# A hybrid decoder step on one core: 54 tiles in the buffer pool in place of 53, and weights kept 4 casts and 3 splits ahead in two stages

## The chip, the cores and the metric

One NeuronCore of a Trainium2 chip. TensorE multiplies, VectorE (DVE) and ScalarE (ACT) do elementwise work, GpSimd (POOL) does little besides issuing DMAs, SyncE (SP) issues most of the loads. Each engine runs its instructions in the order in which they are written; semaphores order the engines among each other. The metric is the device time of one execution in microseconds (us), median of three.

## The reference

One step of a decoder on 1024 prompt tokens and 8 decoding tokens, width 2048, all float32: a pooling layer (A), a key and value projection shared by what follows, and a layer of sliding-window attention (B). Cut to what matters:

```python
def pool_layer(x, prefix, pos, w_in, w_grp, scale, w_out, g_ln, b_ln):
    z = x @ w_in                                    # 2048 -> 4096
    u, gate = z[..., :D_POOL], z[..., D_POOL:]
    d, new_state = multiscale_pool(u, prefix, pos)  # windows 2, 4, 8, 16
    d = jnp.einsum('btgc,gce->btge', d..., w_grp) * scale
    y = (d * jax.nn.silu(gate)) @ w_out
    return layer_norm(ALPHA * x + y, g_ln, b_ln), new_state

kv = h @ w_kv                                       # 4 heads x 64, shared

def attn_layer(x, ...):
    z = x @ w_in                                    # queries and gate
    o = attn_core(rope(q), kb, vb, ..., sinks)      # window 128, a sink per head
    y = (o * jax.nn.silu(gate)) @ w_out
    return layer_norm(ALPHA * x + y, g_ln, b_ln)
```

## The kernel before

**Stages.** The tokens are two chunks: chunk 0 of 512, chunk 1 of 520 (with the 8 decoding tokens). The stages run in the order ai0, ai1 (input of the pooling layer, by chunk), ao0, ao1 (its output), bi0, bi1 (input of the attention layer, with the attention itself woven in), bo0, bo1 (its output). In the profile ai0 lasts to about 388 us, ai1 to 757, ao0 to 914, ao1 to 1080, bi0 to 1536, bi1, the second attention stage, to 1975, bo0, the one behind it, to 2154, and bo1 to the end.

**Products.** A product by a weight block of 128 by 1024 is three matmuls for each of eight slices: a float32 number is split in a high part (ScalarE casts it, L476 for weights, L766 for activations) and a low part (VectorE subtracts, L491 and L775), and high·high (L655), high·low (L656) and low·high (L657) are summed in PSUM. The matmul at L657 is the only one that reads the low part of the weight. Most stages use a form with seven products of block sums in place of eight (Strassen's); the sums of weights are made by VectorE at L334 and written back by GpSimd's DMA (names `swia`, `swob` and so on), so that the second chunk loads them. Two stretches (the first of ai0 and the first of bi0) use plain products (L683 to L685, `unit`).

**Stream of weights.** All weight blocks form one list. Ahead of each product `begin()` writes into the queues what is due: `load_to` issues loads (on SP) up to a products ahead, `prep_to` the splits up to d ahead, `cast_to` the casts up to b ahead, `make_to` the sums that a cast needs. (a, b, d) is `self.ahead`, and 7, 4, 3 at first. From the last queries of bi1 (L2069) it is 6, 3, 2, until 23 products into bo0 (L2186), where it is 7, 4, 3 again. In bi1, whenever fewer than four tiles of the pool are whole and free, `begin()` itself takes 6, 3, 2.

**Pool.** `Mem` holds 53 tiles of 128 by 1040 float32. `full()` gives a whole tile, `half()` half of one, always the one that has been free longest. A weight, its high and its low part take a tile each, and so do pairs of activations.

**Side work.** What isn't a product of the stream is written between products by generators: `x_tick` loads, casts and splits the activations of the next stage, `sum_gen` makes sums of the weights of later stages (L424, L428, L429), others do layer norm (L1277, L1288, L1289), the residual (L1234) and attention. `x_tick` and `sum_gen` go by the number of free tiles: so the size of the pool sets where in the queues their instructions stand. The attention's scores are copied from PSUM (L1793, L1838), masked (L1797 with an int32 mask `mki`; L1839 with a float one in `cst`) and used by L1776, L1829, L1853. L594, L600, L603, L609, L615 and L628 are ScalarE's copies of finished products out of PSUM, L616 and L621 VectorE's.

**Constants.** `cst` holds an identity, a mask, a matrix of 1/D and reciprocal counts, loaded at the start in one DMA, with `mki`.

Of the kernel before, what the change touches and what calls it, by code (L numbers as in the profile page):

```python
# [46 lines left out]
K_ID, K_MP, K_J, K_RC = 0, 128, 256, 384  # L47
N_CST = 384 + 4 * NST
# [15 lines left out]
NSLOT = 53  # L64
# [71 lines left out]
class Mem:  # L136
# [21 lines left out]
    def half(self):  # L158
        part = [(a if b is None else b, i) for i, (a, b) in enumerate(self.f) if (a is None) != (b is None)]
        if part and min(part)[0] > self.clock - 6 and len(self.whole()) > 7:  # L160
            part = []
        i = min(part)[1] if part else min(self.whole(), key=lambda i: max(self.f[i]))
# [4 lines left out]
        return Slot(self, i, h, self.t[i][:, h * TMAX : (h + 1) * TMAX])  # L167
# [15 lines left out]
class Kern:  # L183
    def __init__(self, ctx, tc, io):
# [87 lines left out]
    def load1(self, s, k, src):  # L272
        def go():
            s[k] = self.mem.full()
            self.nc.sync.dma_start(s[k].a[:, :1024], src)

        return go
# [42 lines left out]
    def first_pair(self, name, q):  # L320
# [8 lines left out]
        def add(out, x, y, i):  # L329
            def go():  # L330
                assert self.prepped >= self.made - 2
                if out not in s:
                    s[out] = self.mem.full()
# [68 lines left out]
    def sum_gen(self, name):  # L402
# [8 lines left out]
        def load(n):  # L411
            if n < len(parts) and n not in held:
                q, cs = parts[n]
                s = held[n] = self.mem.full()
# [71 lines left out]
    def prep_to(self, n):  # L486
        self.cast_to(n)
        while self.prepped < min(n, len(self.stream)):
            s = self.stream[self.prepped]
            hi, lo = self.hl[self.prepped], self.mem.full()  # L490
# [76 lines left out]
    def seven(self, c, z0, z1, after, c11=None, split=False, own=None):  # L567
# [30 lines left out]
        def p2():  # L598
            o["s"] = self.mem.half()
# [122 lines left out]
    def t_first(self, j):  # L722
# [5 lines left out]
        if k == 0:  # L728
            for i in (1, 2, 3, 6):
                self.pre[i, g] = self.mem.full(), self.i  # L730
# [9 lines left out]
    def x_load(self):  # L740
# [4 lines left out]
        s = self.mem.full()  # L745
# [13 lines left out]
    def x_cast(self, k):  # L759
# [5 lines left out]
        h = self.mem.full()  # L765
# [3 lines left out]
    def x_make(self):  # L769
# [4 lines left out]
        l = self.mem.full()  # L774
# [42 lines left out]
    def t_ops(self, E, O, dst, kp, TH):  # L817

        nc = self.nc
        s = self.mem.full()  # L820
# [9 lines left out]
    def t_gen(self, key):  # L830
# [3 lines left out]
        def load(kp):  # L834
            s[kp] = self.mem.full()
# [14 lines left out]
    def j_steps(self, T, a, b, box, *free):  # L850

        def add():
            box["u"] = self.mem.half()
# [4 lines left out]
        def high():  # L858
            box["hl"] = self.mem.full()
            self.nc.scalar.copy(box["hl"].r[:, :T], box["u"].a[:, :T])  # L860

        def low():
            u, hl = box.pop("u"), box["hl"]
            self.nc.vector.tensor_sub(hl.r[:, TMAX : TMAX + T], u.a[:, :T], hl.a[:, :T])
# [4 lines left out]
    def j_sum(self, T, box, out):  # L869

        J, hl = self.jr[:], box.pop("hl")
        src = hl.r[:, :T], hl.r[:, TMAX : TMAX + T]
# [11 lines left out]
    def j_sum32(self, T, src, out):  # L884

        J = self.cst[:, K_J : K_J + P]
# [22 lines left out]
    def ln_gen(self, c, pre, acc, gc, bc, out, td):  # L909
# [6 lines left out]
        L = self.mem.full()  # L916
        mu, rr = L.a[:, :T], L.a[:, TMAX : TMAX + T]

        def load(p):
            if p < 8 and p not in pre:  # L920
                pre[p] = self.mem.full()
# [27 lines left out]
        w = self.mem.full()  # L949
        q, v = w.a[:, :T], w.a[:, TMAX : TMAX + T]  # L950
        if c == 0:
            nc.vector.tensor_mul(q, mu, mu)
        else:
            sq, sqs = self.mem.full(), {}
            for p in range(10):
# [4 lines left out]
                if 1 <= p <= 8:  # L960
                    sqs[p - 1] = sq if p == 1 else self.mem.full()
# [50 lines left out]
    def pool_tile(self, c, m, Us, ext, dd):  # L1012
# [13 lines left out]
        bufs = [self.mem.full() for _ in range(2 if w > 2 else 1)]  # L1026
# [10 lines left out]
        if c == 0:  # L1037
            o = K_RC + g * NST
# [15 lines left out]
        def rest():  # L1054
            d = self.mem.full()
            hl = d.r[:, :T], d.r[:, TMAX : TMAX + T]
# [7 lines left out]
    def group_half(self, c, g, h, dd, sg):  # L1064
# [30 lines left out]
        def post():  # L1095
            G = self.mem.full()
# [18 lines left out]
    def two(self, T):  # L1115
# [3 lines left out]
        def z(i):  # L1119
            def go():  # L1120
                if "s" not in box:
                    box["s"] = self.mem.full()
# [6 lines left out]
    def phase_ai(self, c, gs, nxt):  # L1129
# [4 lines left out]
        for g in gs:  # L1134
            ext = es = None
            if T > TP:
                es = self.mem.half()
# [3 lines left out]
            for i in range(4):  # L1141
                if not self.strassen:

                    def done(ps, i=i):
                        U = self.mem.full()
# [4 lines left out]
                elif i % 2 == 0:  # L1150
                    us = {}

                    def z(j, us=us):
                        def go():
                            us[j] = self.mem.full()
# [17 lines left out]
            for i in range(4):  # L1173
                if g == gs[-1] and i == 0:
                    self.x_begin(nxt)
                if not self.strassen:

                    def done(ps, i=i):
                        if i % 2 == 0:
                            sg[i // 2] = self.mem.full()  # L1180
# [1167 lines left out]
```

## Time and profile before

| what | value |
| --- | --- |
| median of three runs | 2343.66 us (2342.93 to 2345.91) |
| the profiled execution: its own time, its span | 2347.06 us, 2345.3 us |
| TensorE busy | 2303.4 us, 98% |
| VectorE, ScalarE, GpSimd busy | 1923.2 (82%), 1364.5 (58%), 204.1 (9%) |
| matmuls in all | 19960 |
| moved by DMA | 669.39 MB, mean 285 GB/s |

A row of a group reads: line, engine, operation, what is written <- what is read, shapes, xcount, then busy us and mean ns of one, then idle time of the engine just ahead of them and what ended most of it. `m` is any tile of the pool, `pD`, `pS`, `pO` are PSUM tiles. A row of waits reads: the engine and line that waited, what ended the wait, total us, times, longest. In a timeline the first number is the start, the second the duration, the bracket the idle time ahead.

### The profile page before, as it was taken

To read this page: it belongs to the slowest core of one execution; us is meant where nothing else is said; L and a number is where in the kernel's file an instruction comes from. 1 tells how busy PE (TensorE), PEld (TensorE's weight loads), DVE (VectorE), ACT (ScalarE), POOL (GpSimd) and SP (SyncE) were. 2 spreads that over 40 slices of the span, in tenths; PEclk is the share of its full clock that TensorE was granted. 3 is DMA by queue.
4 is the path that set the end of the run, shared out by engine and by line. 5 is a ranking of instruction groups with operands and counts; after the bars stand their busy time and mean duration, and the time that the engine had idled before them with its cause. 6 is when DMAs were issued, how large, how long until landed. Compare 5 with 4: busy or idle time off the path is not lost. (4 is left out here: it accounts for less than half of the span.)

```text
span 2345.3 us, 49654 instructions
## 1 busy us (share of the span) xinstructions
PE 2303.4 (98%) x19960; PEld 2204.5 (94%) x19960; DVE 1923.2 (82%) x2382; ACT 1364.5 (58%) x2502; POOL 204.1 (9%) x383
## 2 busy tenths in 40 slices
PE   8999999999999999999999999999999999999997
PEld 6899999999999999998787899999999999999997
DVE  8788898777878878868998898887777777888897
ACT  4454446544546557554464666685666768556666
POOL 0111110010000000000111111100000000000001
PEclk9999999999999999999999999999999999999999
DMA  7668789989889989999799766788776768699794
GB/s 295 211 242 309 269 289 343 339 281 323 297 297 334 321 289 331 316 337 331 260 327 360 256 229 227 246 290 273 251 253 227 240 201 289 228 354 370 264 343 173
DMA packets 252072, 669.39 MB, mean 285 GB/s; under 512 B 25760, under 2 KB 106560, under 8 KB 251840
## 3 DMA queue, kind: packets, MB, share of 16 engines
q1 hardware_dynamic: 206368, 501.14, 63.1%
q0 software_dynamic: 45472, 165.07, 18.1%
q8 instruction: 156, 2.56, 0.4%
q14 instruction: 76, 0.62, 0.1%
HBM read 471.01 MB, written 185.59 MB: 280 GB/s over the span
## 5 line engine op out<-in xcount | busy, mean ns | idle before, releaser
L655 PE MATMUL pD<-m,m 128*128 128x260 f32 (+1 forms) x4752 | 1349.0, 284 | 4.6 <-ACT pD L594 2.8
L657 PE MATMUL pD<-m,m 128*128 128x260 f32 (+1 forms) x4752 | 1343.1, 283 | 7.4 <-DVE m L491 7.3
L656 PE MATMUL pD<-m,m 128*128 128x260 f32 (+1 forms) x4752 | 1342.5, 283 | 1.1 <-DVE m L775 1.1
L655 PEld LDWEIGHTS pD<-m,m 128*128 128x128 f32 x4752 | 897.3, 189 | 13.4 <-issue 5.1
L491 DVE TENSOR_TENSOR m<-m,m 128x1024 fp32r<-128x1024 f32 x674 | 814.8, 1220 | 115.1 <-ACT m L476 66.8
L657 PEld LDWEIGHTS pD<-m,m 128*128 128x128 f32 x4752 | 897.8, 189 | 10.0 <-DVE m L491 9.8
L656 PEld LDWEIGHTS pD<-m,m 128*128 128x128 f32 x4752 | 897.4, 189 | 1.7 <-DVE m L775 1.3
L476 ACT CAST m<-m 128x1024 fp32r<-128x1024 f32 x674 | 703.4, 1049 | 259.1 <-DVE m L334 70.0
L683 PE MATMUL pD<-m,m 128*128 128x512 f32 x448 | 179.9, 402 | 8.0 <-ACT m L766 8.0
L684 PE MATMUL pD<-m,m 128*128 128x512 f32 x448 | 177.4, 396 | 0.6 <-DVE m L775 0.5
L685 PE MATMUL pD<-m,m 128*128 128x512 f32 x448 | 177.4, 396 | 0.0
L775 DVE TENSOR_TENSOR m<-m,m 128x1024 fp32r<-128x1024 f32 (+1 forms) x120 | 147.1, 1227 | 6.5 <-ACT m L766 4.9
L766 ACT CAST m<-m 128x1024 fp32r<-128x1024 f32 (+1 forms) x120 | 125.7, 1052 | 14.1 <-PE pD L684 5.2
L683 PEld LDWEIGHTS pD<-m,m 128*128 128x128 f32 x448 | 84.8, 189 | 29.3 <-ACT m L766 8.0
L334 DVE TENSOR_TENSOR m<-m,m 128x1024 f32<-128x1024 f32 x88 | 107.6, 1222 | 5.7 <-DMA m<-in_wia 4.2
L684 PEld LDWEIGHTS pD<-m,m 128*128 128x128 f32 x448 | 84.9, 189 | 20.4 <-DVE m L775 1.7
L685 PEld LDWEIGHTS pD<-m,m 128*128 128x128 f32 x448 | 84.7, 189 | 19.7
L616 DVE TENSOR_TENSOR m<-pD,m 128x260 f32<-128x260 f32 (+1 forms) x86 | 36.1, 419 | 80.2 <-ACT pD L615 73.6
L628 ACT COPY m<-pD 128x260 f32<-128x260 f32 (+1 forms) x83 | 30.9, 373 | 121.3 <-PE pD L657 121.3
L1812 ACT ACTIVATE m<-m,sm 128x128 f32<-128x128 f32 x256 | 99.3, 391 | 0.0
L1085 PE MATMUL pD<-m,m 128*128 128x260 f32 (+1 forms) x528 | 91.5, 323 | 0.0
L1825 ACT ACTIVATE m<-m,sm 128x128 f32<-128x128 f32 x256 | 81.8, 392 | 12.8 <-DVE sm L1820 12.8
(247 smaller groups left out, 2111.1 us busy)
## 6 DMA issues: line engine op xcount, KB each, us to landing
m<-in_wia SPq DMA_DIRECT2D x124, 512.0 KB
m<-in_wib SPq DMA_DIRECT2D x120, 512.0 KB
swia<-m POOLq DMA_DIRECT2D x64, 512.0 KB, 4.3
m<-swia SPq DMA_DIRECT2D x64, 512.0 KB
m<-swoa SPq DMA_DIRECT2D x64, 512.0 KB
swib<-m POOLq DMA_DIRECT2D x64, 512.0 KB, 5.2
m<-swib SPq DMA_DIRECT2D x64, 512.0 KB
m<-swob SPq DMA_DIRECT2D x56, 512.0 KB
```

Source lines behind the costliest of these rows:

```text
L334: self.nc.vector.tensor_add(s[out].a[:, :1024], s[x].a[:, :1024], s[y].a[:, :1024])
L476: self.nc.scalar.copy(hi.r[:, :1024], self.stream[self.cast].src().a[:, :1024])
L491: self.nc.vector.tensor_sub(lo.r[:, :1024], s.src().a[:, :1024], hi.a[:, :1024])
L655: nc.tensor.matmul(ps[:, :TH], wh[:, s], h, start=new and k == 0, stop=False, skip_group_check=on)
L656: nc.tensor.matmul(ps[:, :TH], wh[:, s], l, start=False, stop=False, skip_group_check=on)
L657: nc.tensor.matmul(ps[:, :TH], wl[:, s], h, start=False, stop=k == 7, skip_group_check=on)
L683: nc.tensor.matmul(ps[:], wh[:, s], h, start=par == 0 and k == 0, stop=False)
L684: nc.tensor.matmul(ps[:], wh[:, s], l, start=False, stop=False)
L685: nc.tensor.matmul(ps[:], wl[:, s], h, start=False, stop=par == 1 and k == 7)
L766: self.nc.scalar.copy(h.r[:, :n], s.a[:, :n])
L775: self.nc.vector.tensor_sub(l.r[:, :n], s.a[:, :n], h.a[:, :n])
L1812: nc.scalar.activation(x["s3"][:, i, :], x["s3"][:, i, :], AF.Exp, bias=nm[:, i : i + 1], scale=0.125, accum_out=rs[:, i : i + 1],)
```

## The change

- The pool has 54 tiles: 52 of 1040 columns and two narrow ones of 1024. `full(n)` and `half(n)` are told how many columns are needed; weights, their sums and parts, and activations of chunk 0 fit into a narrow tile. Pairs that lay at column 1040/2 now lie at column T.
- Space for it: the constants shrink (`cst` 444 columns to 257, the int32 mask is the same memory as the float mask read as int32, `nsink` is computed in place, and the small tiles `carry`, `qd`, `sgd`, `kdec` and a small one of the last stage are parts of one tile, `area`). The matrix of 1/D is made at the start (GpSimd fills, ScalarE copies to `jr`). The identity and the counts are loaded at the start, the mask later, in ao0, over the place of the counts.
- From the last queries of bi1 on, `ahead` is 6, 4, 3; and in bi1 `begin()` falls back to 6, 3, 2 only with fewer than three free tiles.

```diff
-NSLOT = 53
+NSLOT, NWIDE = 54, 52
...
     def new(self, i):
         self.n += 1
-        self.t[i] = self.pool.tile([P, 2 * TMAX], F32, tag=f"m{i}", name=f"m{i}_{self.n}")
+        w = 2 * TMAX if i < NWIDE else 1024
+        self.t[i] = self.pool.tile([P, w], F32, tag=f"m{i}", name=f"m{i}_{self.n}")
...
-    def full(self):
-        i = min(self.whole(), key=lambda i: max(self.f[i]))
+    def full(self, n=2 * TMAX):
+        i = min((i for i in self.whole() if i < NWIDE or n <= 1024), key=lambda i: max(self.f[i]))
...
-        self.mki = one.tile([P, P], I32, name="mki")
+        self.mki = self.cst[:, K_MP : K_MP + P].bitcast(I32)
         self.jr = one.tile([P, P], F32R, name="jr")
-        self.nsink = one.tile([P, NH], F32, name="nsink")
-        self.carry = one.tile([P, NK, NST], F32, name="carry")
-        self.kdec = one.tile([P, 2, NDEC], F32, name="kdec")
-        self.qd = [one.tile([P, NDEC, 8], F32, name=f"qd{i}") for i in range(2)]
-        self.sgd = [one.tile([P, 8, NDEC], F32, name=f"sgd{i}") for i in range(2)]
+        self.nsink = self.prm[:, C_SINK : C_SINK + NH]
+        self.area = one.tile([P, 4 * 64 + 16], F32, name="area")
...
@@ cast_to, and likewise the split, the sums and the loads of weights @@
-            hi = self.mem.full()
+            hi = self.mem.full(1024)
...
@@ begin @@
-        if getattr(self, "ph", "") == "bi1" and len(self.mem.whole()) < 4:
+        if getattr(self, "ph", "") == "bi1" and len(self.mem.whole()) < 3:
             a, b, d = min(a, 6), min(b, 3), min(d, 2)
...
@@ x_cast, and likewise the split of x @@
-        h = self.mem.full()
+        h = self.mem.full(n)
...
@@ the last queries of bi1 @@
                 if c == 1:
-                    self.ahead = 6, 3, 2
+                    self.ahead = 6, 4, 3
...
@@ start @@
+        nc.gpsimd.memset(self.area[:, :P], 1.0 / D)
+        nc.scalar.copy(self.jr[:], self.area[:, :P])
         self.load_to(1)
...
         nc.sync.dma_start(self.prm[:], io["prm"])
-        nc.sync.dma_start(self.cst[:], io["cst"])
-        nc.sync.dma_start(self.mki[:], io["mki"])
+        nc.sync.dma_start(self.cst[:, :P], io["id"])
+        nc.sync.dma_start(self.cst[:, K_MP : K_MP + 4 * NST], io["rc"])
...
-        self.at(9, lambda: nc.scalar.copy(self.jr[:], self.cst[:, K_J : K_J + P]))
...
@@ run, in ao0 @@
+                self.at(1, lambda: self.nc.sync.dma_start(self.cst[:, K_MP:], io["mask"]))
```

How this moves rows is seen on VectorE. Lines below 500 stand 7 lower in the changed program and those behind up to 7: L334 is L341 there, L491 is L498, L1234 is L1241, L1277 is L1284, L1797 is L1803, L775 is L782, L616 and L621 are L623 and L628.

The first place is in bo0, the rows that the trace has from 2050 to 2058 us. Before:

```order
2084 L621 TENSOR_TENSOR m_2641_24657<-pD_24531,m_2545_23778 128x256
2085 L491 TENSOR_TENSOR m_2647_24729<-m_2631_24562,m_2646_24700 128x1024
2086 L334 TENSOR_TENSOR m_2636_24604<-m_2631_24562,m_2636_24604 128x1024
2087 L334 TENSOR_TENSOR m_2631_24562<-m_2631_24562,m_2637_24606 128x1024
2088 L1234 SCALAR_TENSOR_TENSOR m_2641_24657<-m_2619_24414,m_2641_24657 128x1024
2089 L491 TENSOR_TENSOR m_2651_24767<-m_2637_24606,m_2648_24731 128x1024
2090 L1277 TENSOR_TENSOR m_2641_24657<-m_2641_24657,m_2635_24595 128x1024
```

And now:

```order
2084 L498 TENSOR_TENSOR m_2647_24699<-m_2633_24563,m_2645_24660 128x1024
2085 L341 TENSOR_TENSOR m_2638_24603<-m_2633_24563,m_2638_24603 128x1024
2086 L341 TENSOR_TENSOR m_2633_24563<-m_2633_24563,m_2639_24605 128x1024
2087 L628 TENSOR_TENSOR m_2643_24656<-pD_24532,m_2547_23777 128x256
2088 L498 TENSOR_TENSOR m_2649_24732<-m_2639_24605,m_2648_24701 128x1024
2089 L1241 SCALAR_TENSOR_TENSOR m_2643_24656<-m_2621_24417,m_2643_24656 128x1024
2090 L498 TENSOR_TENSOR m_2653_24766<-m_2633_24563,m_2650_24734 128x1024
```

The two sums stood behind the drain of a product (L621) and now stand ahead of it; the split of the third sum (row 2089 before, 2088 now) stood behind L1234 and now stands ahead of it.

The second place is in bi1, around the scores' mask, the rows that the trace has from 1772 to 1785 us. Before:

```order
1818 L1862 SCALAR_TENSOR_TENSOR m_2298_21041<-pO_20950,m_2226_20216 128x512
1819 L428 TENSOR_TENSOR m_2279_20830<-m_2279_20830 128x256
1820 L429 TENSOR_TENSOR m_2279_20830<-m_2279_20830 128x256
1821 L1797 COPY_PREDICATED m_2299_21048<-mki,pS_12831 128x1024
1822 L1801 TENSOR_REDUCE sm_21102<-m_2299_21048 128x8
1823 L1804 SCALAR_TENSOR_TENSOR sm_21103<-sm_21102,nsink 128x8
1824 L1805 TENSOR_TENSOR sm_21104<-sm_21103,nsink 128x8
1825 L491 TENSOR_TENSOR m_2305_21117<-m_2281_20836,m_2297_21015 128x1024
1826 L491 TENSOR_TENSOR m_2306_21119<-m_2287_20888,m_2304_21115 128x1024
```

And now:

```order
1820 L1868 SCALAR_TENSOR_TENSOR m_2299_21042<-pO_20958,m_2227_20218 128x512
1821 L431 TENSOR_TENSOR m_2286_20885<-m_2286_20885 128x512
1822 L498 TENSOR_TENSOR m_2304_21061<-m_2283_20839,m_2298_21016 128x1024
1823 L1803 COPY_PREDICATED m_2300_21049<-cst,pS_12826 128x1024
1824 L1807 TENSOR_REDUCE sm_21107<-m_2300_21049 128x8
1825 L1810 SCALAR_TENSOR_TENSOR sm_21108<-sm_21107,prm 128x8
1826 L1811 TENSOR_TENSOR sm_21109<-sm_21108,prm 128x8
1827 L435 TENSOR_TENSOR m_2286_20885<-m_2286_20885 128x256
1828 L436 TENSOR_TENSOR m_2286_20885<-m_2286_20885 128x256
```

Ahead of the masked copy (L1797, now L1803) there stands one split more, and the sums of L428 and L429 stand behind it.

The third place is at the end of ai0's products, the rows that the trace has from 345 to 352 us. Before:

```order
340 L334 TENSOR_TENSOR m_425_3638<-m_424_3636,m_425_3638 128x1024
341 L616 TENSOR_TENSOR m_433_3704<-pD_3587,m_423_3634 128x256
342 L491 TENSOR_TENSOR m_437_3740<-m_417_3589,m_436_3710 128x1024
343 L334 TENSOR_TENSOR m_424_3636<-m_417_3589,m_424_3636 128x1024
344 L334 TENSOR_TENSOR m_417_3589<-m_417_3589,m_425_3638 128x1024
```

And now:

```order
340 L341 TENSOR_TENSOR m_426_3634<-m_425_3632,m_426_3634 128x1024
341 L782 TENSOR_TENSOR m_437_3732<-m_415_3577,m_432_3696 128x1040
342 L623 TENSOR_TENSOR m_433_3698<-pD_3581,m_424_3630 128x256
343 L498 TENSOR_TENSOR m_439_3738<-m_417_3583,m_436_3704 128x1024
344 L341 TENSOR_TENSOR m_425_3632<-m_417_3583,m_425_3632 128x1024
345 L341 TENSOR_TENSOR m_417_3583<-m_417_3583,m_426_3634 128x1024
```

A split of x for chunk 1 (L775, now L782) stands between them, ahead of the drain; before, it stood 13 rows further back.

More of the change, by code (lines that the diff above doesn't have):

```diff
@@ L156, in full, with half @@
         return Slot(self, i, None, self.t[i][:])
[L158 to L159 removed]
+    def half(self, n=TMAX):
+        fits = lambda i: i < NWIDE or n <= 512
+        part = [
+            (a if b is None else b, i) for i, (a, b) in enumerate(self.f) if (a is None) != (b is None) and fits(i)
+        ]
         if part and min(part)[0] > self.clock - 6 and len(self.whole()) > 7:
             part = []
[L162 removed]
+        i = min(part)[1] if part else min((i for i in self.whole() if fits(i)), key=lambda i: max(self.f[i]))
         h = 0 if self.f[i][0] is not None else 1
@@ L1025, in pool_tile @@
             nc.scalar.copy(ext[:, i, :, 15], U[:, NST + TP : NST + T])
-        bufs = [self.mem.full() for _ in range(2 if w > 2 else 1)]
+        bufs = [self.mem.full(NST + T) for _ in range(2 if w > 2 else 1)]
         src, step, n = U, 1, 0
@@ L1449, in moments @@
             mb, vb = R[0]
-            w, h, S = self.mem.full(), self.mem.full(), [self.mem.half() for _ in range(4)]
+            w, h, S = self.mem.full(), self.mem.full(), [self.mem.half(T) for _ in range(4)]
             m, v, qq, r = (t.a[:, :TH] for t in S)
@@ L1643, in kv_open @@
         if c == 0:
-            self.kv = [self.mem.full() for _ in range(4)]
+            self.kv = [self.mem.full(1024) for _ in range(4)]
             A, B, C, Dd = (s.a for s in self.kv)
@@ L2310 @@
     arrays["prm"] = prm
-    arrays["cst"], arrays["mki"] = _consts()
+    arrays["id"], arrays["mask"], arrays["rc"] = _consts()
     for c, tab in enumerate(_rope_tables()):
```

134 lines of the change are left out of this document (68 added, 66 removed).

## The prediction

> **What bounds the kernel now.** I read the page first, then the waits of TensorE over the whole run, then the same waits stage by stage, and behind each of them the timeline of the engine waited for.
>
> ```profile
> span 2345.3 us, 49654 instructions
> PE 2303.4 (98%) x19960; PEld 2204.5 (94%) x19960; DVE 1923.2 (82%) x2382; ACT 1364.5 (58%) x2502; POOL 204.1 (9%) x383
> L657 PE MATMUL pD<-m,m 128*128 128x260 f32 (+1 forms) x4752 | 1343.1, 283 | 7.4 <-DVE m L491 7.3
> ```
>
> TensorE is busy for 98% of the span. The matmuls are neither removed nor made shorter, so a gain can only come out of the time in which TensorE stands. These are its waits over the span (line that waits, what it waits for, total in us, times, longest):
>
> ```profile
> PE pD L683 <- ACT m L766: 8.0, 1, 8.0
> PE pD L657 <- DVE m L491: 7.3, 11, 1.5
> PE pS L1776 <- DVE m L1746: 4.3, 4, 1.7
> PE pD L655 <- ACT pD L594: 2.8, 2, 1.9
> PE pD L643 <- ACT m L628: 2.4, 1, 2.4
> PE pD L656 <- DVE m L775: 1.1, 1, 1.1
> PE pD L655 <- ACT pD L615: 0.9, 1, 0.9
> PE pD L684 <- DVE m L775: 0.5, 1, 0.5
> ```
>
> The row that the change aims at is the second: 7.3 us in 11 waits for a weight split (L491) that came late. Even if all 11 went, that is 0.3% of the time. Of the 7.3 us, the second attention stage (1536.5 to 1974 us) holds one wait and the output stage behind it (1975.7 to 2100 us) four, with one wait of the score product L1853 among them:
>
> ```profile
> PE pD L657 <- DVE m L491: 1.0, 1, 1.0
> ...
> PE pD L657 <- DVE m L491: 2.5, 4, 1.4
> PE pS L1853 <- DVE m L1839: 0.7, 1, 0.7
> ```
>
> **The change part by part.** No instruction of the weight stream is added or dropped. What moves is the product ahead of which each is written into the in-order queues of ScalarE and VectorE.
>
> *Second attention stage: -1.0.* The rows of VectorE around its one wait:
>
> ```profile
> 1779.42 1.34 DVE L1797 COPY_PREDICATED m<-mki,pS 128x1024 f32<-128x1024 int32 x1 [5.80 <-PE pS L1947]
> 1780.79 1.22 DVE L1801 TENSOR_REDUCE sm<-m 128x8 f32<-128x1024 f32 x1
> 1782.33 2.54 DVE L491 TENSOR_TENSOR m<-m,m 128x1024 fp32r<-128x1024 f32 x2
> ```
>
> VectorE stood 5.80 us at L1797, waiting for scores, with two splits queued behind it. In the new order one more split stands ahead of L1797, where it fits into those 5.80 us at 1.2 us. The split that TensorE lacked then comes one row sooner, by 1.2 us, more than the wait of 1.0. Cover: the idle 5.80 us; without it the 1.0 stays.
>
> *Output stage, chunk 0: -3.2, of which I take 0.8 back.* Every split from the last queries of the attention stage until 23 products into the output stage is written one product earlier, so it may run later by one product than now before TensorE feels it. A product's 24 matmuls take 2.8 us (35.00 us for 298 in the stretch from 2065, below). The four waits sum to 2.5 and the one at L1853 is 0.7, 3.2 in all. The longest, 1.4, is read from these rows:
>
> ```profile
> 2050.59 1.22 DVE L491 TENSOR_TENSOR m<-m,m 128x1024 fp32r<-128x1024 f32 x1
> 2051.72 2.48 DVE L334 TENSOR_TENSOR m<-m,m 128x1024 f32<-128x1024 f32 x2
> 2054.12 1.22 DVE L1234 SCALAR_TENSOR_TENSOR m<-m,m 128x1024 f32<-128x1024 f32 x1
> 2055.25 1.22 DVE L491 TENSOR_TENSOR m<-m,m 128x1024 fp32r<-128x1024 f32 x1
> ```
>
> Two weight sums (L334) and a residual sum (L1234), 3.53 us together (2051.72 to 2055.25), stood ahead of the split of 2055.25. With the split a product nearer the front, L1234 stands behind it (1.13 by the step from 2054.12 to 2055.25), and the sums ahead of it are started in the product before. L1839 (0.7) is freed because the two sums ahead of it move out of its block too. VectorE must then do the same work in 3.2 us less. Whether it can, and whether weights come in time, is in the stretches (us, TensorE, its loads, VectorE, ScalarE, GpSimd, clock, DMA share, GB/s):
>
> ```profile
> 2010.00:2040.00 30.00, 28.34 (x274) 27.14 (x271) 23.19 (x34) 13.71 (x28) 2.82 (x6) 1.00 0.61 217
> 2040.00:2065.00 25.00, 23.45 (x218) 22.87 (x217) 24.05 (x24) 13.91 (x18) 3.62 (x7) 1.00 0.95 334
> 2065.00:2100.00 35.00, 35.00 (x298) 35.00 (x297) 28.85 (x40) 17.98 (x26) 3.19 (x6) 1.00 0.96 354
> 2120.00:2150.00 30.00, 29.23 (x246) 28.82 (x245) 24.24 (x23) 20.55 (x28) 1.06 (x2) 1.00 1.00 368
> 2150.00:2175.00 25.00, 24.68 (x204) 24.35 (x203) 25.00 (x24) 18.51 (x25) 0.53 (x1) 1.00 1.05 393
> ```
>
> From 2010 to 2040 VectorE idles 6.8 us and the DMA engines 39%: room for the earlier sums. From 2040 on both are full (24.05 of 25; 0.95 to 1.05), and the loads are still issued 6 products ahead. ScalarE from 2100 to 2175:
>
> ```profile
> ACT m L476 <- DMA m<-swob: 7.4, 6, 1.8
> ACT m L476 <- DMA m<-in_wob: 4.7, 5, 1.8
> ```
>
> Eleven casts wait there for a weight on its way, so the last products before 2175 run at the pace of the transfers. What TensorE gains before 2040 moves the issue of those transfers too; what it gains between 2049 and 2057 (1.4 and a small wait of 0.2, 1.6 in all) moves TensorE towards a stream that is already full. Bounds of the give-back: nothing (the transfers start earlier by as much) and 1.6; I take the middle, 0.8.
>
> [...]
>
> *First stage, end of chunk 0: +1.1.* One more free tile lets the generator of activations run sooner. One split of x (L775) and its cast move five products forward, ahead of the next two weight sums. There VectorE has no time (first the two waits, then the stretch, then rows of VectorE):
>
> ```profile
> PE pD L655 <- ACT pD L594: 1.9, 1, 1.9
> PE pD L657 <- DVE m L491: 1.5, 1, 1.5
> ...
> 334.00:358.70 24.70, 23.23 (x197) 23.02 (x196) 23.52 (x30) 12.46 (x21) 2.23 (x5) 1.00 0.90 313
> ...
> 346.74 1.23 DVE L334 TENSOR_TENSOR m<-m,m 128x1024 f32<-128x1024 f32 x1 [0.20 <-DMA m<-in_wia]
> ...
> 358.23 1.23 DVE L775 TENSOR_TENSOR m<-m,m 128x1040 fp32r<-128x1040 f32 x1
> 359.38 1.22 DVE L491 TENSOR_TENSOR m<-m,m 128x1024 fp32r<-128x1024 f32 x1
> ```
>
> VectorE is busy for 23.52 of 24.70 us, and the hole of 0.20 us lies ahead of the sum at 346.74, which is ahead of the new place. So the split that TensorE waits for (1.5) comes later by one L775, 1.15 from 358.23 to 359.38, and ScalarE's chain behind it, which ends in the 1.9, shifts with it. Time added is paid at once, since TensorE has nothing else. Bounds: 0 (if the moved split finds a hole I don't see) to 1.15; I take 1.1.
>
> *First attention stage, plain products: +0.6.* A sum of L424 moves ahead of L1746, for which L1776 waits (one of the four in 4.3):
>
> ```profile
> 1144.50:1158.00 13.50, 12.01 (x91) 9.62 (x97) 12.54 (x16) 7.19 (x9) 1.94 (x4) 1.00 0.74 256
> ...
> 1157.15 0.68 DVE L424 TENSOR_TENSOR m<-m 128x512 f32<-128x512 f32 x1
> 1157.75 1.22 DVE L281 TENSOR_TENSOR m<-m,m 128x1024 f32<-128x1024 f32 x1
> ```
>
> It takes 0.60 us (1157.15 to 1157.75) of a VectorE that is busy for 12.54 of 13.5 us, with its hole at the front of the stretch. Bounds 0 and 0.6; I take 0.6.
>
> *First attention stage, the switch to the seven-product form: -0.5.* At 1336 us VectorE stood for a copy of ScalarE:
>
> ```profile
> DVE m L1839 <- ACT m L1838: 1.6, 1, 1.6
> ...
> 1358.20:1361.60 3.40, 3.40 (x19) 3.40 (x18) 3.37 (x5) 0.97 (x6) 0.00 (x0) 0.50 0.34 136
> ...
> 1535.70:1539.10 3.40, 3.40 (x17) 3.40 (x17) 3.40 (x4) 3.40 (x12) 0.00 (x0) 0.50 1.04 398
> ```
>
> A cast of x no longer stands ahead of that copy, so the hole closes by the length of one cast, no more than 1.6, and the waits behind it (L615's 0.9, L775's 1.1) shrink. Bounds 0 and -0.9; I take -0.5.
>
> *Start: -0.3.* 197 KB less of constants (444 and 128 columns of 4 bytes on 128 partitions before; 128 and 60 now) at 393 GB/s, the fastest stretch above, is 0.5 us, as much as the wait of L684; the 8.0 before it ends with x, which comes first. Bounds 0 and -0.5. The mask now comes in a stage with slack, and the other sums and splits that move (some 40) land where TensorE runs 0.9 to 14 us behind their results: nothing, and each would cost up to its own 0.4 to 1.2 us if that cover were gone. Smaller tiles cost no engine anything; sharing one tile for small arrays could add waits, but their writers lie stages apart.
>
> Sum: -1.0 - 3.2 + 0.8 + 1.1 + 0.6 - 0.5 - 0.3 = **-2.5 us**. The profiled execution took 2347.06 us, 1.76 beside its span, and is 3.4 above the median. That is twice 1.7, what a stretch of 3.4 us at a granted clock of 0.50 costs, and it has two such stretches (rows above), each right behind one of the long waits. So I set the sum on the median: 2343.66 - 2.5 = **2341.2**. With all bounds the good way it is -1.0 - 3.2 - 0.9 - 0.5 = -5.6 (2338.1), all the other way -1.0 - 1.6 + 1.75 = -0.9 (2342.8).
>
> **Rivals.**
>
> *The slow clock goes as well.* Each half-clock stretch comes only behind a wait of 1.9 us or more (0.9 and 1.1 in a row; 2.4). If the first is shortened below what the gate reacts to, 1.7 us more are gained. Together with no give-back (0.8) and half of the wait of 1.1 at the start of the next output chunk that splits also cause, it is -2.5 - 1.7 - 0.8 = -5.0, with that half -5.5: 2338.2. For it: the stretches lie at the waits that move. Against: three runs differ by 3 us on one program, so the gate's moment is partly chance. [...]
>
> *Casts run into weights.* Loads stay 6 ahead while casts go to 4: their distance falls from three products to two, 2.8 us of cover lost. Both queues are in order, so a cast that waits for a weight holds every copy out of PSUM behind it (L594, L615, L628), and TensorE waits for those. What is seen from 2100 to 2175, 7.4 us in six waits, would then come in the output stage from 1975 on and reach TensorE: -2.5 + 3.2 - 0.8 + 7.4 = +7.3, **2351.0**. It decides once weights there land less than one product, 2.8 us, ahead of their cast. Against: ScalarE's waits from 1975 to 2100 name no weight now, and the DMA share is only 0.61 in the stretch ahead of 2040.
>
> *Nothing is left.* The pool falls under the new threshold as often, or the full DMA queue takes all back: -3.2 becomes -1.0 or less, and the two losses of 1.7 eat the rest: 2343.7 to 2344.5.
>
> **How the numbers follow.** A measurement of this kernel can tell about 0.2%, 4.7 us, from no change. The forecast (0.50) lies at 2338 to 2343; its better end and the scatter of 3 us make 0.13 of it faster by over 0.2% (below 2339.0), 0.37 the same. The clock rival 0.28: 0.26 faster, 0.02 same. The casts 0.14: 0.12 slower, 0.02 same. Nothing left 0.08: 0.07 same, 0.01 slower. Together faster 0.39, same 0.48, slower 0.13. The range must leave out little of either rival: from 2335.5, the clock rival less part of the scatter, to 2348.5, half of the way to the casts' price.
>
> **What would show it.** Right: no wait of L657 for L491 between 1780 and 1790 and none from 2020 to 2060; VectorE's hole ahead of L1797 one split shorter; the waits at 357 and 1157 us longer by 1.1 and 0.6; casts waiting for weights earlier than 2100 us but not before 2040. Wrong: ScalarE waiting for in_wob or swob between 1960 and 2040 with L655 waiting behind it; the waits of 2150 to 2175 grown by more than 1.6; the waits at 357 us unchanged.

## The result and the profile after

The changed kernel takes 2332.16 us (median of 6 runs, 2329.57 to 2334.33), beside 2344.89 us (6 runs) of the kernel before: a ratio of 0.9945, interval 0.9935 to 0.9955, or 12.7 us less. Run again beside the experiments it gave 2331.5 us and 0.9943 (0.9930 to 0.9957). The forecast was 2.5 us less, with a lower bound of 2335.5: the direction was right, the size was not, and the time lies outside the range.

The page of the changed kernel, the lines that answer to those of before:

```profile
span 2327.8 us, 49646 instructions
PE 2297.9 (99%) x19960; PEld 2201.7 (95%) x19960; DVE 1922.3 (83%) x2382; ACT 1362.7 (59%) x2502; POOL 204.0 (9%) x384
L664 PE MATMUL pD<-m,m 128*128 128x260 f32 (+1 forms) x4752 | 1339.6, 282 | 5.5 <-DVE m L498 5.4
```

And the waits of TensorE in it, in the same columns as before (L664 was L657, L498 was L491, L662 was L655, L650 was L643, L782 was L775, L1782 was L1776):

```profile
PE pD L690 <- ACT m L773: 8.1, 1, 8.1
PE pD L664 <- DVE m L498: 5.4, 7, 2.9
PE pD L1504 <- POOL area L1530: 1.3, 1, 1.3
PE pD L650 <- ACT m L635: 1.0, 1, 1.0
PE pD L662 <- ACT pD L601: 0.9, 1, 0.9
PE pD L662 <- ACT m L635: 0.8, 1, 0.8
PE pD L663 <- DVE m L782: 0.6, 1, 0.6
PE pD L691 <- DVE m L782: 0.5, 1, 0.5
```

The row that the forecast looked at, the late weight split, lost only 1.9 of 7.3 us. The row of the scores' product, 4.3 us in four waits for L1746, is gone (in a second execution one wait of 1.0 stands in bi1, and none in bi0), and no part of the forecast had touched it but to make it longer. Both programs run the same 19960 matmuls, so the start of the k-th in one trace beside the k-th in the other says where the time went. Two executions of the changed kernel against the profiled one of before (us; negative is earlier):

| stretch of the kernel before | changed | changed, again | forecast |
| --- | --- | --- | --- |
| start to 343 | -0.1 | -0.3 | -0.3 |
| 343 to 388, end of ai0 | +0.8 | +0.2 | +1.1 |
| 388 to 1122, ai1, ao0, ao1 | -0.9 | -0.9 | 0 |
| 1122 to 1182, bi0, first two waits of L1776 | -1.7 | -1.4 | +0.6 |
| 1182 to 1353 | -1.0 | -1.0 | 0 |
| 1353 to 1363, the switch in bi0 | -3.2 | -3.0 | -0.5 |
| 1363 to 1544, end of bi0 | -4.6 | -1.8 | 0 |
| 1544 to 1974, bi1 | -1.9 | -0.8 | -1.0 |
| 1974 to 2078, bo0 | -4.2 | -4.1 | -3.2 |
| 2078 to 2175, start of bo1 | +0.1 | -0.3 | +0.8 |
| 2175 to the end | -0.8 | -0.8 | 0 |
| sum | -17.4 | -14.3 | -2.5 |

The sums are larger than the 12.7 of the medians because the profiled execution of before, with its two half-clock stretches (3.41 us each at a granted clock of 0.50, from 1358.20 and 1535.69 us), was one of the long ones (2347.06), and the first profiled one of the changed kernel was the shortest (2329.57). Some 10 of the 17 us come out of the first attention stage, bi0, where the forecast had +0.6 and -0.5; 3.4 of the 10 are those two half-clock stretches, by half of their length. Two places in bi0 show a cause. The first is at 1144 us. VectorE in the kernel before, ahead of the layer norm's centred sums (idle time in the bracket):

```profile
1144.58 0.43 DVE L976 TENSOR_SCALAR m<-pO 128x260 f32<-128x260 f32 x1 [3.29 <-PE pO L880]
...
1146.05 0.70 DVE L902 TENSOR_TENSOR m<-m 128x520 f32<-128x520 f32 x1 [0.70 <-ACT m L901]
...
1156.54 0.69 DVE L1746 TENSOR_TENSOR m<-m,m 128x512 f32<-128x512 f32 x1
```

And in the changed one:

```profile
1141.93 0.43 DVE L983 TENSOR_SCALAR m<-pO 128x260 f32<-128x260 f32 x1 [0.46 <-PE pO L887]
1142.27 0.42 DVE L983 TENSOR_SCALAR m<-pD 128x260 f32<-128x260 f32 x1
...
1154.48 0.69 DVE L1752 TENSOR_TENSOR m<-m,m 128x512 f32<-128x512 f32 x1
```

VectorE stood for 3.29 us until TensorE's sum over channels (L880) came, and then ran, but for one hole of 0.70 us that stays in the changed kernel, to the late L1746. Now that sum stands twelve matmuls, half a plain product, earlier in TensorE's own queue. TensorE before, and changed:

```profile
1144.14 0.40 PE L880 MATMUL pO<-m,jr 128*128 128x260 f32 x2
```

```profile
1141.49 0.40 PE L887 MATMUL pO<-m,jr 128*128 128x260 f32 x2
```

VectorE takes it up 2.65 us earlier, and L1746 (now L1752) is done at 1155.2 in place of 1157.2. The sum of L424 stands ahead of it as forecast and costs its 0.6, out of a gain of 2.65.

The second place is at 1517 us. ScalarE before, and behind it the same copy in the changed kernel:

```profile
1517.33 0.37 ACT L600 COPY m<-pD 128x256 f32<-128x256 f32 x1 [3.82 <-DMA to<-m]
```

```profile
1506.78 0.35 ACT L607 COPY m<-pD 128x256 f32<-128x256 f32 x1
```

The copy out of PSUM was to go into a tile whose old content was still on its way to memory (`to`). It stood 3.82 us, and with it everything behind it on ScalarE, among it the copy of the scores (L1838) on which L1746's stretch hangs. With a tile more, the one free longest is another, and the copy waits for nothing.

### The profile page after: what moved, and what is told of

It reads as the page before. It is cut to its first block, busy times and chain, and to the rows that moved or that the text cites. A ratio compares the mean times of both kernels' runs of the same rounds, so it can differ in the third digit from the quotient of the medians.

```text
span 2327.8 us, 49646 instructions
## 1 busy us (share of the span) xinstructions
PE 2297.9 (99%) x19960; PEld 2201.7 (95%) x19960; DVE 1922.3 (83%) x2382; ACT 1362.7 (59%) x2502; POOL 204.0 (9%) x384
## 5 line engine op out<-in xcount | busy, mean ns | idle before, releaser
L662 PE MATMUL pD<-m,m 128*128 128x260 f32 (+1 forms) x4752 | 1345.7, 283 | 1.8 <-ACT pD L601 0.9
L664 PE MATMUL pD<-m,m 128*128 128x260 f32 (+1 forms) x4752 | 1339.6, 282 | 5.5 <-DVE m L498 5.4
L662 PEld LDWEIGHTS pD<-m,m 128*128 128x128 f32 x4752 | 895.5, 188 | 9.6 <-issue 5.5
L664 PEld LDWEIGHTS pD<-m,m 128*128 128x128 f32 x4752 | 895.9, 189 | 7.2 <-DVE m L498 7.1
L663 PEld LDWEIGHTS pD<-m,m 128*128 128x128 f32 x4752 | 895.6, 188 | 1.3 <-DVE m L782 0.8
L498 DVE TENSOR_TENSOR m<-m,m 128x1024 fp32r<-128x1024 f32 x674 | 814.6, 1220 | 96.2 <-ACT m L483 62.6
L691 PE MATMUL pD<-m,m 128*128 128x512 f32 x448 | 177.4, 396 | 0.5 <-DVE m L782 0.5
L782 DVE TENSOR_TENSOR m<-m,m 128x1024 fp32r<-128x1024 f32 (+1 forms) x120 | 147.0, 1227 | 10.3 <-ACT m L773 8.7
L341 DVE TENSOR_TENSOR m<-m,m 128x1024 f32<-128x1024 f32 x88 | 107.6, 1223 | 9.1 <-DMA m<-in_wia 6.8
L690 PEld LDWEIGHTS pD<-m,m 128*128 128x128 f32 x448 | 84.8, 189 | 29.4 <-ACT m L773 8.1
L623 DVE TENSOR_TENSOR m<-pD,m 128x260 f32<-128x260 f32 (+1 forms) x86 | 36.2, 421 | 83.8 <-ACT pD L622 76.3
L691 PEld LDWEIGHTS pD<-m,m 128*128 128x128 f32 x448 | 84.9, 189 | 20.0 <-DVE m L782 1.0
L692 PEld LDWEIGHTS pD<-m,m 128*128 128x128 f32 x448 | 84.8, 189 | 19.7
L1818 ACT ACTIVATE m<-m,sm 128x128 f32<-128x128 f32 x256 | 99.3, 391 | 0.0
L1092 PEld LDWEIGHTS pD<-m,m 128*128 128x128 f32 x528 | 79.4, 188 | 8.1
```

The lines of the kernel that those rows point to most:

```text
L341: self.nc.vector.tensor_add(s[out].a[:, :1024], s[x].a[:, :1024], s[y].a[:, :1024])
L498: self.nc.vector.tensor_sub(lo.r[:, :1024], s.src().a[:, :1024], hi.a[:, :1024])
L662: nc.tensor.matmul(ps[:, :TH], wh[:, s], h, start=new and k == 0, stop=False, skip_group_check=on)
L663: nc.tensor.matmul(ps[:, :TH], wh[:, s], l, start=False, stop=False, skip_group_check=on)
L664: nc.tensor.matmul(ps[:, :TH], wl[:, s], h, start=False, stop=k == 7, skip_group_check=on)
L690: nc.tensor.matmul(ps[:], wh[:, s], h, start=par == 0 and k == 0, stop=False)
```

## The experiments

Theory A: the extra tile, by letting side work run sooner and by other tiles being the oldest, takes most of the gain; depth takes what bo0 shows. The rival B: depth takes all.

**Depth and threshold without the tile**, on the kernel before:

```diff
-        if getattr(self, "ph", "") == "bi1" and len(self.mem.whole()) < 4:
+        if getattr(self, "ph", "") == "bi1" and len(self.mem.whole()) < 3:
...
-                    self.ahead = 6, 3, 2
+                    self.ahead = 6, 4, 3
```

> The kernel before with 6, 4, 3 at the last queries of the second attention stage and the threshold of three free tiles; no extra tile. Theory A (the extra tile moves side work in the first attention stage and takes most of the gain; the depth of casts and splits is worth what the second attention stage and the output stage behind it showed, 1.8 and 4.2 us): 3 to 6 us faster, about 2340 us; the waits of the score product L1776 for L1746 in the first attention stage stay at 4.3 us. Rival B (depth is the source of all): 11 to 13 us faster, about 2332 us. Rival C (depth without the tile runs out of tiles): no gain or slower, and loads that wait for tiles.

Measured: 2344.94 us, 0.9996 (0.9987 to 1.0004): no change. B has fallen; A's 3 to 6 us didn't come either. Its waits of TensorE in bi1 (first fence) and bo0 (second):

```profile
PE pD L657 <- DVE m L491: 1.8, 1, 1.8
PE pO L1853 <- DVE m L1839: 0.8, 1, 0.8
```

```profile
PE pD L655 <- ACT m L628: 1.2, 1, 1.2
```

In bo0 all five waits for L491 and L1839 are gone, 4.2 us by the starts of the matmuls. But bi1's waits grew from 1.4 to 2.6, and the first product of bo0 waits 1.2 in place of 0.5 for ScalarE: depth without room gives back part of what it brings. By the starts of the matmuls 2.6 us of gain are left behind bi0, which the timed runs don't confirm (at most 3.0 by the interval).

**The tile and the constants alone** (6, 3, 2 and the threshold of four in the changed kernel):

```diff
-        if getattr(self, "ph", "") == "bi1" and len(self.mem.whole()) < 3:
+        if getattr(self, "ph", "") == "bi1" and len(self.mem.whole()) < 4:
...
-                    self.ahead = 6, 4, 3
+                    self.ahead = 6, 3, 2
```

> The changed kernel with 6, 3, 2 and the threshold of four as before: the extra tile and the smaller constants alone. Theory A: 7 to 9 us faster than the kernel before, about 2337 us, with no wait of L1776 for L1746 left in the first attention stage and the waits for L491 in the output stage back at about 2.5 us. Rival B: within 2 us of the kernel before. Rival C: the whole gain of 12 to 13 us.

Measured: 2339.97 us, 0.9976 (0.9966 to 0.9985), 5.4 less. Short of A's 7 to 9, for a reason that its waits show, in bi1 and in bo0:

```profile
PE pD L664 <- DVE m L498: 1.8, 1, 1.8
PE pO L1859 <- DVE m L1845: 1.4, 1, 1.4
```

```profile
PE pD L664 <- DVE m L498: 2.5, 4, 1.3
PE pS L1859 <- DVE m L1845: 0.7, 1, 0.7
PE pD L662 <- ACT m L635: 0.5, 1, 0.5
```

bi0 is as in the changed kernel (9.7 us earlier at its end, 10.7 there), bo0 as before, and bi1 3.3 us longer than before, 1.7 of them a half-clock stretch at 1777 us, right behind the wait of 1.8. The two parts measured alone give 0.4 and 5.4, and all together 12.7: they aren't independent. The smaller constants were never run without the tile, so "the tile" stands for both here and below.

**Tile and threshold, without the depth** (the changed kernel with 6, 3, 2):

```diff
-                    self.ahead = 6, 4, 3
+                    self.ahead = 6, 3, 2
```

> The changed kernel with 6, 3, 2 from the last queries on: tile, constants and the threshold of three, without the depth. Theory H (with the extra tile it is the threshold that pays in the second attention stage, and the depth alone in the output stage): the second attention stage 1.5 to 2 us shorter than before, as in the changed kernel, the output stage behind it as before with its waits of 2.5 and 0.7: 4 to 5 us slower than the changed kernel, about 2336.5 us. Rival D (the depth repairs the second attention stage too): its waits of 1.4 and 1.8 us from the run without both are there, and it is 7 to 8 us slower, about 2340 us.

Measured: 2335.48 us, 0.9961 (0.9949 to 0.9974). Theory H holds: TensorE waits for nothing in bi1, while bo0 still has its 2.4 and 0.7. By the ratios to the kernel before, of 2345 us: the tile alone 5.6 us, within some 2; the threshold on top of it 3.5 and the depth on top of both about 4, which are differences of two ratios and by their intervals uncertain by some 3 to 4 us each. The depth's share is the firmer of these two: the five runs without it (2335.14 to 2337.34) all lie above the five of the changed kernel beside them (2329.76 to 2334.25).

**The layer norm's step.** In `end()`, side work steps if `room >= self.room`; the free tiles are 5 in the changed kernel and 4 in the one before at one single event where 5 are asked for, number 377 in bi0. Held to its old place in the changed kernel, and let in early in the kernel before:

```diff
-... and room >= self.room:
+... and room >= self.room and self.i != 377:
```

> The changed kernel, but the step of the layer norm that the fifth free tile lets in (the sum over channels, L880, half a product earlier) is held to its old place; nothing else moves. Theory A1 (this one step frees the waits of L1776 at 1157 and 1181 us, 1.5 and 0.4): the two waits are back, 1.5 to 2.5 us slower than the changed kernel, about 2334 us. Rival A2 (those waits went for another reason, the sums and splits that moved): the waits stay gone and the time is that of the changed kernel, within 0.5 us at this place.

```diff
-... and room >= self.room:
+... and (room >= self.room or self.i == 377):
```

> The kernel before with that one step half a product earlier; nothing else moves. Theory A1: the waits of L1776 at 1157 and 1181 us go, 1.9 us less in the trace at this place, 2342 to 2343 us. Rival A2: both waits stay and the time is that of the kernel before.

Measured: held late, 2336.21 us (4 runs, 0.9957, 0.9943 to 0.9971), 3 to 4 us behind the changed kernel; early, 2341.37 us, 0.9981 (0.9972 to 0.9990), 4 us ahead of the kernel before. The waits of TensorE from 1100 to 1200 us in the kernel held late, and, from 1130 to 1190, in the one before and in the one with the early step:

```profile
PE pS L1706 <- ACT m L2031: 2.8, 1, 2.8
PE pS L1782 <- DVE m L1752: 2.1, 1, 2.1
```

```profile
PE pS L1776 <- DVE m L1746: 1.9, 2, 1.5
```

```profile
PE pS L1700 <- ACT m L2025: 0.9, 1, 0.9
```

A1 holds in both directions for the wait of 1.5 at 1157 us: four matmuls moved by half a product carry it. The wait of 0.4 at 1181 us went with the early step but didn't come back in the kernel held late, so its cause is open. Both timed differences are larger than the 1.9 us at the place. The early kernel also lost the third wait of L1776 at 1288 us (0.8 by the starts). The late one took two half-clock stretches in its profile, 1.7 us each (the mean clock from 1131 to 1137 us is 0.72), one of them right behind the returned wait; the other follows the wait of 2.8 for L2031 at 1128 us, ahead of the step that the edit moves. That wait (L1700 in the kernel before, L1706 in the changed one) comes and goes: 0.2 and 0.5 in two executions of the changed kernel, none in the one before. The profiled execution of the late kernel was its slowest (2341.76), so how much of its 3 to 4 us belongs to the step isn't settled.

**The other tile**, in the kernel before, where ScalarE's copy stood for the DMA:

```diff
-        i = min(part)[1] if part else min(self.whole(), key=lambda i: max(self.f[i]))
+        i = min(part)[1] if part else sorted(self.whole(), key=lambda i: max(self.f[i]))[second]
...
-            o["s"] = self.mem.half()
+            o["s"] = self.mem.half(int(self.i == 487))
```

> The kernel before, in which one ScalarE copy (L600, at 1517 us) takes the tile that has been free second longest instead of the longest; no instruction moves. Theory T (that tile was still being written out by the DMA to the next stage, which held ScalarE for 3.1 to 3.8 us, the score copy L1838 behind it and with it L1776): ScalarE's wait goes, the wait of L1776 at 1525 us (1.2 to 1.7) goes, that of L643 behind it shrinks; 1.2 to 3 us less at this place, with one half-clock stretch of 1.7 us less where one stood there. Rival: ScalarE waits for the second tile as long, or L1776 waits for the splits instead, and nothing is gained.

Measured: 2345.43 us, 1.0002 (0.9993 to 1.0011). The trace and the timed runs don't agree. In the trace the cause holds: the copy has no wait, and of the waits from 1500 to 1536 us, which were 2.4 for L643 and 1.7 for L1776, one is left:

```profile
PE pD L643 <- ACT m L628: 2.4, 1, 2.4
```

L1776's 1.7 us are gone (1.9 by the starts), but L643's stayed and the timed runs show no gain (at most 1.6 by the interval). That the tile held ScalarE and L1776 is shown; that it is worth 1.9 us by itself isn't. L643's wait has another cause, which stays open: it is 0.9 to 2.4 in the profiles with 54 tiles and 1.3 to 2.9 in those with 53.

**The moved split of x** at 350 us, put back in the changed kernel:

```diff
-        free = lambda: len(self.mem.whole())
+        free = lambda: len(self.mem.whole()) - (self.ph == "ai0")
```

> The changed kernel, but in the first stage on chunk 0 the generator of activations counts one free tile less, so that the split of x moves back to its old place. Theory A: the wait for L491 at 358 us falls from 2.9 to 1.5 us while L594's 1.9 behind it comes back, and less half clock: 0 to 2 us faster than the changed kernel. Rival: the split's place doesn't matter, the wait of 2.9 us stays.

Measured: 2332.21 us, 0.9944 (0.9931 to 0.9956). Waits from 340 to 365 us, in this kernel and in the changed one run beside it:

```profile
PE pD L664 <- DVE m L498: 1.3, 1, 1.3
PE pD L662 <- ACT pD L601: 0.9, 1, 0.9
```

```profile
PE pD L664 <- DVE m L498: 2.6, 1, 2.6
PE pD L662 <- ACT pD L601: 0.9, 1, 0.9
```

The split's place is worth 1.3 us in the row of waits, and 1.4 by the starts from 343 to 388 us (forecast: 1.1). The edit also moves a split of x at 81 us, where TensorE waits for nothing. The wait of 1.9 for L594 (now L601), expected to come back, stayed at 0.9. The whole is no faster: bi1 and bo0 of this execution lost it again, in a wait of 0.8 at 1708 us and one of 1.8 at 1963 us, at places that the edit doesn't reorder. Which tile is handed out there does change; whether that is the cause wasn't tried.

The changed kernel unaltered beside it:

> The changed kernel unaltered, beside the three others. All theories: 2331 to 2333 us, as measured before. [...]

It had a half-clock stretch, but at 1528 us behind a wait of 2.3, and none behind the wait of 2.6 at 358.

**All three parts without the tile**, on the kernel before: the early step, the other tile, the depth and the threshold (the diffs above).

> The kernel before, 53 tiles, with the three parts together that were run one by one: the layer norm's step half a product earlier, the other tile for the ScalarE copy at 1517 us, and depth 6, 4, 3 with the threshold of three. Theory S (the gain is a sum of such places, each of which the tile only sets off): the waits of L1776 at 1157, 1181 and 1525 us and those of the output stage are gone together, 4 to 8 us faster than before, 2337 to 2341 us; what is left to the changed kernel, 5 to 8 us, lies in the switch at 1356 us with its half-clock stretch, in the second attention stage and at the very end. Rival P (the free tile itself is what counts, the loads that it lets start): less than 3 us.

Measured: 2340.54 us, 0.9970 (0.9958 to 0.9983), 5.9 less. S holds in size, and so does its remainder: 6 us by the ratios and 8 by the medians to the changed kernel. Its place holds in part: by the starts the changed kernel's first execution is 1.6 us ahead in the switch and 1.8 in bi1, as S had it, but also 3.7 in bo0, which S didn't name. By the starts of the matmuls the depth again costs ahead of bo0, 3.6 us in one wait of 2.5 for L628 at 1970 us with a half-clock stretch behind it. That wait is 0.8 with the tile.

**Loads one product less ahead**, in the changed kernel:

```diff
-                    self.ahead = 6, 4, 3
+                    self.ahead = 5, 4, 3
```

> The changed kernel with the loads 5 products ahead in place of 6 from the last queries on, one product between load and cast where there are two. Theory A (weights land two products or more ahead of their cast until 2075 us, so that this cover is not used up): casts wait for weights by 1 to 3 us more, TensorE by less than 2 us, 2331 to 2334 us. Rival W (the cover is used up, as the forecast's rival of casts that run into weights has it): ScalarE waits for in_wob and swob from 1960 us on, TensorE behind it, 5 us slower or more, 2337 us and above.

Measured: 2337.32 us, 0.9960 (0.9945 to 0.9975), about 4 us behind the changed kernel by the ratios: the size lies between the two theories, its median where W has it. Waits of TensorE from 1950 to 2120 us:

```profile
PE pD L664 <- DVE m L498: 2.3, 1, 2.3
PE pD L662 <- ACT m L635: 2.1, 1, 2.1
PE pS L1782 <- DVE m L1752: 1.7, 1, 1.7
PE pS L1859 <- DVE m L1845: 1.2, 1, 1.2
PE pD L662 <- ACT m L610: 0.6, 1, 0.6
```

And ScalarE's waits for weights from 1950 to 2165 us in this kernel, and those of the first trace of the changed one from 2075 to 2165, ahead of which it has none:

```profile
ACT m L483 <- DMA m<-swob: 5.6, 5, 1.7
ACT m L483 <- DMA m<-in_wob: 3.9, 4, 1.8
ACT m L483 <- DMA m<-swib: 3.3, 1, 3.3
```

```profile
ACT m L483 <- DMA m<-swob: 5.1, 4, 1.8
...
ACT m L483 <- DMA m<-in_wob: 2.4, 3, 1.7
```

12.8 us in place of 7.5: with one product between load and cast more weights come late, and TensorE feels it. The edit isn't clean, though: one split of x and its cast also come earlier, from 1997 to 1945 us, and their share of the 4 us wasn't measured. With two, the change's distance, no cast waits for a weight from 1950 to 2075 us in its first trace (in the second 2.4 us). The forecast's rival of casts that run into weights begins one product beyond the change.

## Why the prediction was wrong

**First attention stage, plain products (+0.6).** This step failed first. It followed VectorE's rows ahead of L1746 and found one sum more there. It didn't follow the hole at the front of that stretch, 3.29 us of waiting for TensorE's L880, to what sets L880's place. The order was compared from product to product, and a plain product is fed in two halves with an event after each: the sum moved by half of one, inside a product, and four matmuls were the only ones of TensorE that moved in the whole program. Measured: -1.7 and -1.4 over both waits, in place of +0.6; holding the step brings the longer one back. The sum that the forecast priced did stand there and cost its 0.6; what was missing is the sum over channels that came 2.65 us sooner.

**"Nothing" from 1363 to 1544 us.** The waits of L1776 (1.7) and L643 (2.4) there were in the quoted row of waits, but not traced back beyond L1746. Behind L1776's stood ScalarE's 3.82 us for a tile still being written out; what sets L643's is open. That a change of the pool changes which tile is handed out, and so such waits, had no term in the sum at all. The runs with 53 tiles that kept the old choice waited there 3.1 to 3.8 us, those with 54 didn't. The row of the table has -4.6 and -1.8: 1.9 in both is L1776's wait, and the rest of the -4.6 is a shorter wait of L643 and the half-clock stretch behind it, which the second execution had as well.

**The switch in bi0 (-0.5).** The mechanism was right, the size wasn't. The two waits of 0.9 and 1.1 became one of 0.6 in the first trace and 0.8 in the second: -1.2 to -1.4 in place of -0.5, beyond the bound of -0.9. With 54 tiles no profile has the half-clock stretch behind them, 1.7 us; with 53 three of five have it. The forecast had that as a rival at 0.28, and there it came as the rival had it: behind the wait of 0.6 the granted clock of the first trace is 1.00.

**Second attention stage (-1.0)** and **output stage (-3.2).** Right in place and kind; all six waits that they name went, and VectorE's hole ahead of the mask shrank from 5.80 us to 3.54. Both were mis-sized. In bi1 the sum had left out a wait of 0.4 for L1839, and the second execution lost 1.0 of its gain again in a wait of L1782. And the terms were sums of wait rows, while a wait here cost more than its row. Two rows of the chain of waits of the kernel before, the matmul right behind the wait of 1.4 and one in steady work:

```profile
2056.52 0.39 PE pD L657
...
2072.04 0.12 PE pD L657
```

The first matmul behind this wait advances the chain by 0.39 in place of 0.12 us. Five waits of 3.2 us in the output stage thus were 4.2 to 4.6 by the starts. The part that the depth has in it is smaller than the forecast had it: in bi1 it is the threshold that takes the waits away, and only with the tile.

**End of ai0 (+1.1).** Right for the split: the wait for it grew by 1.5 (1.5 to 2.9) in one execution and by 1.2 in the other, and putting the split back took 1.4 away. Wrong for what stands behind it: the wait of 1.9 for L594 was to shift along and instead fell to 0.9 or nothing with 54 tiles, for a reason that no run isolates. So the stretch as a whole changed by only +0.2 in the second execution, and by +0.8 in the first with 1.7 of half clock in it.

**Give-back (+0.8).** It didn't come: what bo0 lost against the forecast's stream of weights from 2078 to 2133 (0.4 and 1.1) came back by 2175. The DMA engines were full there before and after (shares of 0.98 from 2078 to 2133 and 1.02 on to 2175 us before, of 0.99 and 1.03 after, 16.7 us earlier), but the loads of `swob` from 2088 to 2165 us were issued 16 to 22 us earlier in the first execution, and TensorE ran 16.7 earlier.

**Start (-0.3).** 0.1 to 0.3 less at 343 us, but not where the forecast had it: the wait of L684 (now L691) stayed at 0.5. That the size fits is luck.

In the traces the net miss is thus some 5 to 7 us of first-attention-stage waits that were not in the sum, 3.4 us of half clock in the profiled execution (less in the medians), and 2 us of waits priced by their rows. Some 0.9 us between 388 and 1122 and 0.8 behind 2175 have no cause shown here. In the timed runs it splits another way: the tile gave 5.6 us where its terms (+1.1, +0.6, -0.5, -0.3) came to 0.9 lost, and threshold and depth on top of it 7 where theirs (-1.0, -3.2, +0.8) came to 3.4.

## What to carry to other kernels

A pool size is an input of every decision that counts free tiles: list the events at which the count crosses a bound, on all engines and inside products, before looking at the edit that the change is named after. Follow each wait of the bounding engine back to the first hole on the engine behind it, and ask whether that hole is a tile not yet free. And price parts together: here depth and threshold alone were worth nothing that could be measured, the tile alone 5 us, all together 13.

## What the runs showed of the hardware

In the traces of the two kernels the half-clock stretches lie on a grid of 3.41 us. In the kernel before, the two among the products last 3.41 us each at a granted clock of 0.50; they start at 1358.20 and 1535.69 us, 177.49 us apart, which is 52 steps of 3.4133. Behind the last product the clock is at 0.50 again from 2337.82 us, 979.62 behind the first, 287 of these steps. In the first trace of the changed kernel it is at 0.50 for 3.41 us from 359.46 us and again from 2322.13, 1962.67 later, 575 of them.

In the steps of this grid right ahead of the three stretches TensorE idled 1.99 and 2.38 us (before) and 2.49 us (changed). The last of these (TensorE busy 0.92 of 3.46 us, then the stretch at 0.50):

```profile
356.00:359.46 3.46, 0.92 (x7) 0.92 (x8) 3.39 (x7) 2.04 (x4) 0.00 (x0) 1.00 1.02 406
359.46:362.87 3.41, 3.41 (x18) 3.41 (x17) 3.41 (x4) 3.41 (x5) 0.00 (x0) 0.50 1.08 385
```

Of the steps with no half-clock stretch behind them, from 15 us to the last matmul, the one with the most idle time has 1.55 us in the kernel before (from 1522.04 us) and 1.32 in the changed one (from 2311.89). No fixed bound is shown: in the kernel with the other tile 1.69 us of idle time had the stretch behind them (busy 1.72 of 3.41 us from 1353.46, clock 0.50 from 1356.87), in the one with the three parts without the tile 1.75 us had none (busy 1.65 of 3.40 us from 1527.30, then clock 1.00).

How a wait lies on the grid may count as well: the wait of 1.9 for L594 in the kernel before put 1.48 us into the step from 358.09 us and 0.40 into the next, and the clock stayed at 1.00. In two executions of the changed kernel the stretch fell on other waits: in one at 359 us, in the other at 1528 us and not behind the 2.6 at 358.

So in these runs a half-clock stretch cost 1.7 us on top of the wait ahead of it (3.41 us at a clock of 0.50). This is why the switch in bi0, where two waits of 2.0 us together became one of 0.6 or 0.8, gained 3.2 and 3.0 us. It may also be a part of why one and the same kernel spreads over several us (2329.57 to 2334.33 for the changed one); the runs without a profile don't show that.
